# Encoder kernel, first layer: parts of w_in as one listed sequence, own buffers for early modulations, squares summed over pairs, splits one unit ahead

## The chip, the cores and the metric

One Trainium2 chip, one core of it, no communication. The metric is the time of one execution in device microseconds. The engines are TensorE (PE, matmuls; its weight loads are listed as PEld), VectorE (DVE), ScalarE (ACT), GpSimd (POOL) and SyncE (SP), whose queue issues all loads and stores.

## What is computed

Two layers of a bidirectional encoder for 256 tokens of width 2048, all in float32. Each layer modulates, mixes with two kinds of attention, gates, and runs a gated MLP with a short convolution. Cut to what matters:

```python
mod = silu(c) @ ada_w[l] + ada_b[l]                  # 2048 -> 6 x 2048: shift, scale, gate, twice
h = rmsnorm(x, norm_mix[l]) * (1.0 + sc_a) + sh_a
qa, ka, va, qb, kb, vb, ga, gb = split_cols(h @ w_in[l])      # 8704 columns
ya = window_attention(norm_rot(qa), norm_rot(ka), va, sink) @ w_proj_a[l]
yb = neighbourhood_attention(norm(qb), norm(kb), vb, bias) @ w_proj_b[l]
x = x + gt_a * ((sigmoid(ga) * ya + sigmoid(gb) * yb) @ w_out[l])
h = rmsnorm(x, norm_ffn[l]) * (1.0 + sc_m) + sh_m
g, v = split(depthwise_conv(h @ w_up[l]))
x = x + gt_m * ((silu(g) * v) @ w_down[l])
```

## The kernel before

**Weights.** All weights of a layer lie in one stream of 128 x 128 blocks in the order in which they are used (`block_stream`, line 74). Sixteen blocks are a unit, 1 MB. `unit` (L248) loads a unit (L253) into one of four `raw` tiles and splits each half of it into a high part (a cast to fp32r on ACT, L262) and a low part (a subtraction on DVE, L263); the two go into an `hl` tile, of which there are four, so two units. Every product is three matmuls: high x high, high x low, low x high. `Stream.next_block` (L292) asks for a unit when its first block is wanted.

**Two kinds of products.** `tokens` (L319) multiplies the 256 tokens with four neighbouring blocks of one row chunk: matmuls of 512 columns into two PSUM tiles, L329 to L331. `features` (L303) multiplies one block at a time, 256 columns, L271 to L273. The pool `mm` holds four PSUM tiles, the pool `ax` three more for everything else.

**Modulations.** `ada` (L184) makes one 128-wide piece of a modulation per step: a load of 1 MB (L193), which takes a `raw` tile too, and a fused multiply and sum on DVE (L194). There are 96 per layer; the first 32 are the shift and scale of the first h, in pairs by chunk of 128 channels. When both pieces of a chunk are there, `normed` (L415) makes that chunk of h: a product `ht` on DVE (L421), the high part on ACT (L424), the low part on DVE (L425). `plan` (L643) tells by a table of corners how many modulations are to be done when a unit of the stream ends.

**The first layer's start.** The sum of squares of x is made at L671 to L683: four squares on ACT, three adds and two halvings on DVE, two matmuls with a column of 1/D, an add of EPS on DVE. `roots` (L410) raises it to -0.5 on POOL, `spread` turns it into a row for all partitions by two transposes (L403) and a copy (L407): `rbs`, which `ht` needs.

**The first layer's w_in.** It has 13 column groups: nine of 512 columns for q, k and v (`QKV_GROUPS`) and 16 gate blocks of 128, run four rows of chunks at a time. The 16 chunks of the inner dimension are cut into four parts of 2, 4, 5 and 5 chunks (`K_PARTS_0`, L42); each part goes over all column groups before the next begins, so that work can start with two chunks of h. Between parts, sums wait in SBUF (`packs`, `ya`): the first part is copied there on ACT (L819, L855), later ones are added on DVE (L821, L850). A paced job, `ada_and_h` (L656), makes modulations and h chunks at 0.65 steps per unit, and what a part lacks when it begins is made at once (L806).

**Attention.** When a group of q and k is complete, `qk_rows` (L500) normalises it some ticks later; heads run as a paced job (`attention`, L782), whose steps are one per tick times a rate `ATT`. A head is scores (L584), softmax, four transposes (L610), a product with v (L618) and its split into `oA` or `oB`. `w_proj_a` (L862) starts after eight heads of A and reads all eight in each of its outputs.

The framework orders each engine's instructions by priority and by its own estimates; the rows in the section on the change are the outcome.

Of the kernel before, what the change touches and what calls it, by code (L numbers as in the profile page):

```python
# [32 lines left out]


# [84 lines left out]
def encoder(ctx: ExitStack, tc: tile.TileContext, a: dict, out: bass.AP):  # L119
# [25 lines left out]
    nc.vector.memset(mhalf[:], -0.5)  # L145
    def load(src, shape, name, p=const, **kw):
        t = p.tile(shape, F32, name=name, **kw)
        nc.sync.dma_start(t[:], src)
# [33 lines left out]
    mods, amods, nrms, done = {}, {}, {}, {0: 0, 1: 0}  # L182

    def ada(l):  # L184
# [6 lines left out]
        for n, i in enumerate(ADA_ORDER):  # L191
            raw = rawp.tile([P, D], F32, name=f"aw{l}_{n}", tag="raw")
            nc.sync.dma_start(raw[:], a["aw"][l, n])  # L193
            nc.vector.tensor_tensor_reduce(  # L194
                out=raw[:], in0=raw[:], in1=cact[:], scale=1.0, scalar=ab[:, i : i + 1],
# [52 lines left out]
    def unit(l, u):  # L248
# [4 lines left out]
        nc.sync.dma_start(raw[:], a["ws"][l, u])  # L253
# [828 lines left out]
```

## Time and profile before

| | us |
|---|---|
| median of 3 runs | 2689.32 (2689.2 to 2689.62) |
| the profiled execution | 2685.71 |
| its span, first to last instruction | 2683.2 |
| PE busy | 2647.0 |
| DVE busy | 2101.2 |
| ACT busy | 1393.7 |
| mean granted clock of TensorE | 0.997 |

The median is of unprofiled runs; all rows shown are of the profiled execution. A row of a timeline is: start, duration, engine, line, operation, output <- inputs, count, and in brackets the idle time of the engine just before and who ended it. A row of a group is: busy time, mean of one in ns, idle time before. Durations of neighbouring instructions of one engine overlap a little, and matmuls overlap by more than a third, so that the distance of starts, not the duration, is their rate. PE's busy share counts matmuls at reduced clock as busy; the granted clock stands beside it.

### The profile page before, as it was taken

To read this page: it belongs to the slowest core of one execution; us is meant where nothing else is said; L and a number is where in the kernel's file an instruction comes from. 1 tells how busy PE (TensorE), PEld (TensorE's weight loads), DVE (VectorE), ACT (ScalarE), POOL (GpSimd) and SP (SyncE) were. 2 spreads that over 40 slices of the span, in tenths; PEclk is the share of its full clock that TensorE was granted. 3 is DMA by queue.
4 is the path that set the end of the run, shared out by engine and by line. 5 is a ranking of instruction groups with operands and counts; after the bars stand their busy time and mean duration, and the time that the engine had idled before them with its cause. 6 is when DMAs were issued, how large, how long until landed. Compare 5 with 4: busy or idle time off the path is not lost.

```text
span 2683.2 us, 50732 instructions
## 1 busy us (share of the span) xinstructions
PE 2647.0 (99%) x21152; PEld 2559.6 (95%) x21152; DVE 2101.2 (78%) x2964; ACT 1393.7 (52%) x2266; POOL 36.3 (1%) x56
## 2 busy tenths in 40 slices
PE   7899999999999999999999999999999999999999
PEld 5689889999999999999998889999999999999999
DVE  6998988997988888788886666768878866655664
ACT  5344764455753555355554566544565445544553
POOL 0000100000000000000000000000000000000000
PEclk9999999999999999999999999999999999999999
DMA  8887768987688777887756656776747865555554
GB/s 320 333 341 290 269 234 326 357 322 250 233 286 336 291 269 281 325 303 269 294 213 256 242 219 228 245 260 245 291 173 282 300 252 191 196 195 190 193 199 142
DMA packets 104711, 700.40 MB, mean 261 GB/s; under 512 B 13473, under 2 KB 19873, under 8 KB 20513
## 3 DMA queue, kind: packets, MB, share of 16 engines
q1 hardware_dynamic: 104482, 697.18, 71.1%
q8 instruction: 165, 2.70, 0.4%
q14 instruction: 64, 0.52, 0.1%
HBM read 695.03 MB, written 2.10 MB: 260 GB/s over the span
## 4 chain that ended last, share of the span: by engine, by line
PE 92%; DVE 3%; DMA 2%; issue 1%; ACT 1%; POOL 0%; DVEq 0%; ACTq 0%
PE ps L271 25%; PE ps L273 25%; PE ps L272 25%; PE ps_t L330 5%; PE ps_t L331 5%; PE ps_t L329 5%; DMA aw<-in_aw 2%; DVE aw L194 1%; DVE hl L263 1%; PE sc L584 1%; PE po L618 1%; PE tp L610 1%; PE qtp L539 0%; PE cb L157 0%; ACT hl L262 0%
## 5 line engine op out<-in xcount | busy, mean ns | idle before, releaser
L263 DVE TENSOR_TENSOR hl<-w,hl 128x1024 fp32r<-128x1024 f32 x928 | 1127.7, 1222 | 315.4 <-ACT hl L262 314.2
L262 ACT CAST hl<-w 128x1024 fp32r<-128x1024 f32 x928 | 969.4, 1049 | 741.1 <-PE ps L273 446.8
L271 PE MATMUL ps<-h,hl 128*128 128x256 f32 x3328 | 924.5, 278 | 0.0
L273 PE MATMUL ps<-h,hl 128*128 128x256 f32 x3328 | 922.3, 277 | 0.0
L272 PE MATMUL ps<-h,hl 128*128 128x256 f32 x3328 | 921.6, 277 | 0.0
L271 PEld LDWEIGHTS ps<-h,hl 128*128 128x128 f32 x3328 | 626.0, 188 | 0.2
L272 PEld LDWEIGHTS ps<-h,hl 128*128 128x128 f32 x3328 | 625.2, 188 | 0.2
L273 PEld LDWEIGHTS ps<-h,hl 128*128 128x128 f32 x3328 | 625.1, 188 | 0.3 <-DVE hl L263 0.2
L194 DVE CUSTOM_DVE_ANT_0 aw<-aw,cact,ab 128x2048 f32<-128x2048 f32 x192 | 450.9, 2349 | 81.5 <-DMA aw<-in_aw 81.1
L329 PE MATMUL ps_t<-hl,h 128*128 128x512 f32 x576 | 227.7, 398 | 7.6 <-ACT hl L262 7.0
L330 PE MATMUL ps_t<-hl,h 128*128 128x512 f32 x576 | 227.0, 394 | 3.9 <-DVE hl L263 3.9
L331 PE MATMUL ps_t<-hl,h 128*128 128x512 f32 x576 | 226.2, 393 | 0.9 <-DVE h L425 0.9
L927 DVE SCALAR_TENSOR_TENSOR u<-ps,cw,u 128x255 f32<-128x255 f32 x304 | 146.4, 482 | 79.9 <-ACT u L925 75.4
L925 ACT ACTIVATE u<-ps,cw 128x256 f32<-128x256 f32 x152 | 85.6, 563 | 186.9 <-PE ps L273 186.9
L273 PE MATMUL ps<-merged,hl 128*128 128x256 f32 x512 | 141.7, 277 | 0.0
L272 PE MATMUL ps<-merged,hl 128*128 128x256 f32 x512 | 141.6, 277 | 0.0
L271 PE MATMUL ps<-merged,hl 128*128 128x256 f32 x512 | 141.6, 277 | 0.0
L273 PE MATMUL ps<-act_o,hl 128*128 128x256 f32 x512 | 141.5, 276 | 0.0
L272 PE MATMUL ps<-act_o,hl 128*128 128x256 f32 x512 | 141.5, 276 | 0.0
L271 PE MATMUL ps<-act_o,hl 128*128 128x256 f32 x512 | 141.2, 276 | 0.0
L329 PEld LDWEIGHTS ps_t<-hl,h 128*128 128x128 f32 x576 | 109.2, 190 | 31.0 <-ACT hl L262 7.6
L330 PEld LDWEIGHTS ps_t<-hl,h 128*128 128x128 f32 x576 | 109.1, 189 | 28.7 <-DVE hl L263 6.1
(213 smaller groups left out, 4579.6 us busy)
## 6 DMA issues: line engine op xcount, KB each, us to landing
w<-in_ws SPq DMA_DIRECT2D x464, 1024.0 KB, 4.9
aw<-in_aw SPq DMA_DIRECT2D x192, 1024.0 KB, 5.3
bias<-in_bias SPq DMA_DIRECT2D x64, 64.0 KB, 3.8
x<-in_xT SPq DMA_DIRECT2D x4, 512.0 KB, 5.2
out<-x SPq DMA_DIRECT2D x16, 128.0 KB, 2.2
cw<-in_cw SPq DMA_DIRECT2D x2, 176.0 KB, 3.2
maskA<-in_maskA SPq DMA_DIRECT2D x1, 256.0 KB, 5.7
ab<-in_ab SPq DMA_DIRECT2D x2, 48.0 KB, 5.4
```

What stands on the lines that cost most here:

```text
L194: nc.vector.tensor_tensor_reduce(out=raw[:], in0=raw[:], in1=cact[:], scale=1.0, scalar=ab[:, i : i + 1], op0=ALU.mult, op1=ALU.add, accum ...
L262: nc.scalar.copy(hl[:, 0], r)
L263: nc.vector.tensor_tensor(out=hl[:, 1], in0=r, in1=hl[:, 0].bitcast(F32), op=ALU.subtract)
L271: nc.tensor.matmul(out, hi, act[:, 0], start=first, stop=False)
L272: nc.tensor.matmul(ps[:, :S], hi, act[:, 1, :S], start=False, stop=False)
L273: nc.tensor.matmul(out, lo, act[:, 0], start=False, stop=last)
L329: nc.tensor.matmul(ps[:], xh, hi, start=kc == kcs[0], stop=False)
L330: nc.tensor.matmul(ps[:], xh, lo, start=False, stop=False)
L331: nc.tensor.matmul(ps[:], xl, hi, start=False, stop=kc == kcs[-1])
L584: nc.tensor.matmul(sc[:, t, :n], qT[:, t * P : (t + 1) * P], seen(t, kT), start=True, stop=True)
L925: nc.scalar.activation(out=u, in_=ps, func=AF.Identity, scale=w[:, 1:2], bias=w[:, 3:4])
L927: nc.vector.scalar_tensor_tensor(out=u[:, to], in0=ps[:, of], scalar=w[:, j : j + 1], in1=u[:, to], op0=ALU.mult, op1=ALU.add)
```

## The change

It concerns the first layer up to `w_proj_a`, and the pacing of modulations and heads.

1. The parts are gone. `ORDER` lists, for the first layer, turns of (column group, chunks to be reached); `turns` makes from it which chunks each turn adds. The gate blocks are four groups of four (groups 9 to 12). Groups reach different depths: the table begins with group 1 over chunks 0 and 1, group 0 over chunk 0, group 4 over 0 and 1, group 2 over 0 to 3; group 6 stops at chunk 1 until near the end. There are 33 turns of q, k and v in place of 36, and 12 turns of four gates in place of 16, so DVE has 48 adds of 512 columns in place of 54 and 32 of 256 in place of 48.
2. `need_h` makes each chunk of h with its two modulations when a turn asks for it, and `plan` makes chunks ahead; the paced job is gone. The corners of the plan now begin at unit 0.
3. The first three modulations of the first layer are loaded into space of `o` and `b1` (`own`), not into `raw` tiles. Unit 0 is issued after two modulations, in two loads of half a unit.
4. The squares of x: two on DVE, two on ACT; POOL adds the first two, DVE the last two; 16 matmuls of one column (8 for each half of the tokens) sum the rest in PSUM, and ACT adds EPS. A small power on POOL (`tried`) runs at the start. On ACT the four steps that make `cact` now stand ahead of the squares.
5. In the first layer up to unit 52 each unit's load and split are issued when the unit before begins (`SPLIT_AHEAD`).
6. The small tables (masks, gains, convolution weights) are loaded when the first group becomes complete, at unit 34, and no longer in the first unit.
7. `ATT` goes from 1.288 to 0.947 steps per tick, `ATT_B` from 0.21 to 0.296; heads of A may start when groups 0 to 2 are ready, heads of B when their own three are. Gates' sums of unfinished turns use `ax` PSUM tiles.

`SEEDED` is empty and `REDUCED` is 0, so the code that they guard is not built. `skip` is smaller by what `eps` and `tried` take, so addresses behind them stay. The instructions of the second layer's w_in and all later stages are the same, apart from where modulations fall among them.

```diff
-K_PARTS_0 = [2, 4, 5, 5]
+GATES = 4
+ORDER = [
+    [
+        (1, 2), (0, 1), (4, 2), (2, 4), (5, 3), (9, 3), (3, 2), (6, 2), (8, 3),
...
+    [(k, KC) for k in range(13)],
+]
-ADA_PLAN_0 = [(38, 32), (58, 48), (76, 66), (84, 70), (98, 80), (108, 80), (128, 88), (142, 99), (176, 113), (193, 126), (219, 136), (231, 143)]
+ADA_PLAN_0 = [(0, 3), (16, 18), (34, 32), (38, 32), (58, 48), (77, 67), (83, 70), (97, 80), (107, 80), (127, 86), (142, 99), (176, 111), (193, 126), (219, 139), (228, 142)]
-FIRST_RATE = 0.65
+OWN = 3
+SPLIT_AHEAD = 52
-ATT = [1.288, 0.4]
+ATT = [0.947, 0.4]
-ATT_B = [0.21, 0.21]
+ATT_B = [0.296, 0.21]
...
+    tried = const.tile([P, 1], F32, name="tried")
+    nc.gpsimd.tensor_tensor(out=tried[:], in0=mean[:], in1=mhalf[:, :1], op=ALU.pow)
...
-            raw = rawp.tile([P, D], F32, name=f"aw{l}_{n}", tag="raw")
+            raw = own.pop(0) if own else rawp.tile([P, D], F32, name=f"aw{l}_{n}", tag="raw")[:]
...
+        pieces = 1 if l or u else 2
...
-                if self.ahead:
-                    self.halves = self.ahead.popleft()
-                else:
-                    self.halves = unit(self.l, self.u)
+                if not self.ahead:
+                    self.prefetch(1)
+                self.halves = self.ahead.popleft()
                 self.u, self.at = self.u + 1, 0
+                if self.l == 0 and self.u < SPLIT_AHEAD:
+                    self.prefetch(1 - len(self.ahead))
...
+        if l == 0:
+            need_h(min(KC, (sum(done.values()) - 1) // 2))
...
+    def need_h(n):
+        while hs_done[0] < n:
+            need(0, 2 * hs_done[0] + 2)
+            next(hs_steps[0])
+            hs_done[0] += 1
...
+        if i < 8:
+            nc.vector.tensor_tensor(out=sq[:], in0=x[:, i : i + 4], in1=x[:, i : i + 4], op=ALU.mult)
+        else:
+            tc.keep_in_program_order(nc.scalar.activation(out=sq[:], in_=x[:, i : i + 4], func=AF.Square))
+        sqs.append(sq)
+    nc.gpsimd.tensor_tensor(out=sqs[0][:], in0=sqs[0][:], in1=sqs[1][:], op=ALU.add)
+    nc.vector.tensor_tensor(out=sqs[2][:], in0=sqs[2][:], in1=sqs[3][:], op=ALU.add)
...
-            todo = [(3, head_a, i) for i in range(HA)] + [(6 + 3 * (i // 4), head_b, i) for i in range(HB)]
+            todo = [({0, 1, 2}, head_a, i) for i in range(HA)]
+            todo += [({3, 4, 5} if i < 4 else {6, 7, 8}, head_b, i) for i in range(HB)]
...
+        for n, (k, kcs) in enumerate(turns(l)):
+            if l == 0:
+                need_h(kcs[-1] + 1)
+            if kcs[-1] == KC - 1 and not waits[0]:
+                gains, sink, cw, rots = small(l)
+                waits[0] = True
```

**How it moves instructions: three places.** First SP's queue at the start, before (`aw0_n` is the n-th modulation's weights, `w0_n` unit n of the first layer):

```order
L193 DMA aw0_0_145<-in_aw 128x2048
L193 DMA aw0_1_148<-in_aw 128x2048
L193 DMA aw0_2_170<-in_aw 128x2048
L193 DMA aw0_3_173<-in_aw 128x2048
L253 DMA w0_0_187<-in_ws 128x2048
L148 DMA maskA_207<-in_maskA 128x512
```

and now (`own_o` and `own_b1` are the modulations' own buffers):

```order
L230 DMA own_o_124<-in_aw 128x2048 x2
L293 DMA w0_0_169<-in_ws 128x1024 x2
L230 DMA own_b1_125<-in_aw 128x2048
L230 DMA aw0_3_202<-in_aw 128x2048
L293 DMA w0_1_212<-in_ws 128x2048
L293 DMA w0_2_252<-in_ws 128x2048
```

Unit 0 has moved ahead of the third and fourth modulation, units 1 and 2 follow at once, and the small tables are gone from here.

Second, DVE's list between the splits (`hl0_u_half`) of unit 6 and unit 7 before, with modulations 7 to 12 and three chunks of h:

```order
L263 TENSOR_TENSOR hl0_6_1_516<-w0_6_511,hl0_6_1_516 128x1024
L194 ISA aw0_7_550,mod0_139<-aw0_7_550,cact_94,ab0_140 128x2048
L194 ISA aw0_8_558,mod0_139<-aw0_8_558,cact_94,ab0_140 128x2048
L194 ISA aw0_9_561,mod0_139<-aw0_9_561,cact_94,ab0_140 128x2048
L194 ISA aw0_10_569,mod0_139<-aw0_10_569,cact_94,ab0_140 128x2048
L194 ISA aw0_11_572,mod0_139<-aw0_11_572,cact_94,ab0_140 128x2048
L194 ISA aw0_12_594,mod0_139<-aw0_12_594,cact_94,ab0_140 128x2048
L263 TENSOR_TENSOR hl0_7_0_599<-w0_7_597,hl0_7_0_599 128x1024
```

and now between the splits of units 2 and 3, and around that of unit 6 (small instructions left out):

```order
L303 TENSOR_TENSOR hl0_2_1_257<-w0_2_252,hl0_2_1_257 128x1024
L231 ISA aw0_4_268,mod0_158<-aw0_4_268,cact_98,ab0_159 128x2048
L231 ISA aw0_5_271,mod0_158<-aw0_5_271,cact_98,ab0_159 128x2048
L231 ISA aw0_6_279,mod0_158<-aw0_6_279,cact_98,ab0_159 128x2048
L231 ISA aw0_7_282,mod0_158<-aw0_7_282,cact_98,ab0_159 128x2048
L303 TENSOR_TENSOR hl0_3_0_312<-w0_3_310,hl0_3_0_312 128x1024
L303 TENSOR_TENSOR hl0_6_0_450<-w0_6_448,hl0_6_0_450 128x1024
L231 ISA aw0_8_470,mod0_158<-aw0_8_470,cact_98,ab0_159 128x2048
L303 TENSOR_TENSOR hl0_6_1_453<-w0_6_448,hl0_6_1_453 128x1024
L231 ISA aw0_9_473,mod0_158<-aw0_9_473,cact_98,ab0_159 128x2048
L303 TENSOR_TENSOR hl0_7_0_497<-w0_7_495,hl0_7_0_497 128x1024
```

The row of six modulations at unit 7 has become a row of four ahead of unit 3, and from there on one or two stand between splits.

Third, PE's list in `w_proj_a` (`ps0_u_..` is an output whose last block lies in unit u, `oA0_6` and `oA0_7` heads 6 and 7, `tp` a head's transposes, `sc` its scores, `po` its product with v). Before:

```order
L610 MATMUL tp_3080<-ident_85,p_3052 128x128
L618 MATMUL po_3183<-pT_3085,vh_2946 128x256 x6
L271 MATMUL ps0_52_16_0_3353<-oA0_6_2968,hl0_52_0_3356 128x256
L271 MATMUL ps0_53_8_0_3387<-oA0_6_2968,hl0_52_1_3359 128x256
L271 MATMUL ps0_53_16_0_3460<-oA0_6_2968,hl0_53_0_3463 128x256
L271 MATMUL ps0_54_8_0_3494<-oA0_6_2968,hl0_53_1_3466 128x256
L610 MATMUL tp_3192<-ident_85,p_3089 128x128
L618 MATMUL po_3305<-pT_3197,vh_2946 128x256 x6
L271 MATMUL ps0_52_16_0_3353<-oA0_7_3070,hl0_52_0_3356 128x256
```

and now:

```order
L311 MATMUL ps0_52_16_0_3326<-oA0_6_2963,hl0_52_0_3329 128x256
L311 MATMUL ps0_53_8_0_3360<-oA0_0_2362,hl0_52_1_3332 128x256
L311 MATMUL ps0_53_8_0_3360<-oA0_6_2963,hl0_52_1_3332 128x256
L662 MATMUL tp_3247<-ident_85,p_3158 128x128
L670 MATMUL po_3283<-pT_3252,vh_2941 128x256 x5
L311 MATMUL ps0_54_8_0_3423<-oA0_0_2362,hl0_53_1_3395 128x256
L311 MATMUL ps0_52_16_0_3326<-oA0_7_3074,hl0_52_0_3329 128x256
```

Before, four outputs were open, all of them short of head 6, when the transposes and the product of head 6 stood in the list, and then again for head 7. Now head 6's product stands ahead of the first output's last blocks, and three outputs are open when head 7 comes.

More of the change, by code (lines that the diff above doesn't have):

```diff
@@ L182, in encoder @@
     mods, amods, nrms, done = {}, {}, {}, {0: 0, 1: 0}
+    own = []
+    for tag, n in (("o", 16), ("b1", 12)):
+        t = place(tag, n, F32, f"own_{tag}").rearrange("p n s -> p (n s)")
+        own += [t[:, i : i + D] for i in range(0, n * S - D + 1, D)]
+    own = own[:OWN]
     def ada(l):
@@ L654, in need @@
             next(adas)
-    def ada_and_h(steps):
-        for kc in range(KC):
-            while done[0] < 2 * kc + 1:
-                next(adas)
-                yield
-            next(adas)
-            next(steps)
-            yield
-    for _ in range(FIRST):
-        next(adas)
-    for i in range(0, KC, 4):
-        nc.sync.dma_start(x[:, i : i + 4], a["xT"][:, i : i + 4])
-    mean_sq = sm.tile([P, 2], F32, name="ms_in", tag="nsa")
-    acc = place("y0", 4, F32, "sq_in")
-    for i in range(0, KC, 4):
-        sq = acc if i == 0 else place(f"y{1 + i // 4 % 2}", 4, F32, f"sq_in{i}")
-        nc.scalar.activation(out=sq[:], in_=x[:, i : i + 4], func=AF.Square)
-        if i:
-            nc.vector.tensor_tensor(out=acc[:], in0=acc[:], in1=sq[:], op=ALU.add)
@@ new lines, in encoder @@
+    nc.gpsimd.tensor_tensor(out=sqs[0][:], in0=sqs[0][:], in1=sqs[1][:], op=ALU.add)
+    nc.vector.tensor_tensor(out=sqs[2][:], in0=sqs[2][:], in1=sqs[3][:], op=ALU.add)
+    pss = [ax.tile([P, 2], F32, name="ss_in", tag="ss", bufs=1), ax.tile([P, 512], F32, name="ss_in1", tag="ax")]
+    for sq in sqs[::2]:
+        for t in range(2):
+            for i in range(4):
+                nc.tensor.matmul(
+                    pss[t][:, :1], sq[:, i, t * P : (t + 1) * P], mean[:],
+                    start=sq is sqs[0] and i == 0, stop=sq is sqs[2] and i == 3,
+                )
@@ L681, in encoder @@
     for t in range(2):
-        nc.tensor.matmul(ps[:, t : t + 1], acc[:, 0, t * P : (t + 1) * P], mean[:], start=True, stop=True)
-    nc.vector.tensor_scalar(out=mean_sq[:], in0=ps[:], scalar1=EPS, scalar2=None, op0=ALU.add)
+        nc.scalar.activation(out=mean_sq[:, t : t + 1], in_=pss[t][:, :1], func=AF.Identity, bias=eps[:])
     tables = []
@@ L746, in va @@
             return vas[g]
-        ready, heads = [0], [0]
+        ready, heads = set(), [0]
         oA, oB = [], []
@@ new lines, in gate, with gate_a @@
+        def gate(n, mo, kcs):
+            first, last = kcs[0] == 0, kcs[-1] == KC - 1
+            apart = l == 0 and not waits[0]
+            seeded = apart and n in SEEDED and not first
+            if not apart:
+                clean[0] = False
+            def gate_a(ps):
+                src = ps
+                if not first and not seeded:
+                    nc.vector.tensor_tensor(out=ya[:, mo], in0=ps, in1=ya[:, mo], op=ALU.add)
+                    src = ya[:, mo]
+                if last:
+                    half_tanh(ya[:, mo], src)
+                elif first or seeded:
+                    nc.scalar.copy(ya[:, mo], ps)
+            st.features([hs[k] for k in kcs], [gate_a], apart=apart, seed=ya[:, mo] if seeded else None)
```

172 lines of the change are left out of this document (97 added, 75 removed), and 4 rows, old and new, of the table ORDER.

## The prediction

> **What bounds the kernel now.** I read the page's first lines, then a table of windows with one row for each stage, then the waits, and for the two stages that lose time the timeline. The page gives the span:
>
> ```profile
> span 2683.2 us, 50732 instructions
> PE 2647.0 (99%) x21152; PEld 2559.6 (95%) x21152; DVE 2101.2 (78%) x2964; ACT 1393.7 (52%) x2266; POOL 36.3 (1%) x56
> aw<-in_aw SPq DMA_DIRECT2D x192, 1024.0 KB, 5.3
> ```
>
> The windows by stage (stretch in us, its length, busy time of each engine with instructions, granted clock, DMA share, GB/s) say where the 36 us are that PE is not busy:
>
> ```profile
> 0.00:26.00 26.00, 11.52 (x26) 6.21 (x26) 13.83 (x19) 10.32 (x13) 3.57 (x7) 1.00 0.93 353
> 26.00:67.00 41.00, 39.12 (x207) 32.99 (x206) 31.49 (x42) 28.15 (x49) 0.00 (x0) 0.96 0.80 298
> 67.00:82.00 15.00, 5.35 (x17) 3.00 (x17) 14.89 (x20) 3.78 (x6) 0.00 (x0) 0.75 0.98 374
> 82.00:276.00 194.00, 193.11 (x1053) 168.18 (x1052) 183.46 (x242) 86.81 (x139) 7.06 (x4) 0.99 0.84 316
> 276.00:349.00 73.00, 72.41 (x479) 64.94 (x478) 71.41 (x139) 56.75 (x150) 7.98 (x4) 1.00 0.70 259
> 349.00:418.00 69.00, 64.39 (x507) 61.22 (x506) 58.57 (x123) 40.19 (x93) 2.08 (x14) 0.98 0.69 250
> 418.00:2683.00 2265.00, 2261.15 (x18876) 2223.07 (x18875) 1727.60 (x2384) 1167.70 (x1821) 15.59 (x28) 1.00 0.70 254
> ```
>
> After 418 us PE idles under 4 us in 2265, and the change leaves the order there nearly alone; the gain or loss is made before. PE idles at the start (no product of w_in before 26), in 67 to 82 (5.35 busy of 15, clock 0.75, while DVE is full with 14.89), and in 349 to 418 (4.6 idle). DVE is nearly full from 67 to 349. The rate of PE, from neighbouring starts, first at full clock and then after the long stop:
>
> ```profile
> 37.24 0.39 PE L329 MATMUL ps_t<-hl,h 128*128 128x512 f32 x1
> 37.47 0.39 PE L330 MATMUL ps_t<-hl,h 128*128 128x512 f32 x1
> ...
> 66.94 0.39 PE L329 MATMUL ps_t<-hl,h 128*128 128x512 f32 x1
> ...
> 69.42 0.39 PE L330 MATMUL ps_t<-hl,h 128*128 128x512 f32 x1
> 69.65 0.39 PE L329 MATMUL ps_t<-hl,h 128*128 128x512 f32 x1
> ...
> 71.21 0.73 PE L331 MATMUL ps_t<-hl,h 128*128 128x512 f32 x2 [0.93 <-DVE h L425]
> 78.93 1.22 PE L329 MATMUL ps_t<-hl,h 128*128 128x512 f32 x2 [6.99 <-ACT hl L262]
> 81.26 0.80 PE L330 MATMUL ps_t<-hl,h 128*128 128x512 f32 x1 [1.11 <-DVE hl L263]
> ...
> 82.71 0.63 PE L331 MATMUL ps_t<-hl,h 128*128 128x512 f32 x1
> 83.14 0.63 PE L329 MATMUL ps_t<-hl,h 128*128 128x512 f32 x1
> ```
>
> A matmul starts every 0.23 us, and every 0.43 after the stop. A unit of 16 blocks has 24 of them: 5.5 us (48 of half the length for gates: the same). The row at 66.94 is the first of the second part, 6.5 units in. From there 17 matmuls (3.9 us) take 15 us, and the next 8 run at half rate: 11.1 + 1.6 = **12.7 us lost**. The cause is the five modulations in a row on DVE.
>
> **The change part by part.** Rows for the prices (line, operation, count, then busy us, mean ns), the last two of POOL and ACT:
>
> ```profile
> L263 DVE TENSOR_TENSOR hl<-w,hl 128x1024 fp32r<-128x1024 f32 x118 | 142.3, 1220 | 14.3 <-ACT hl L262 14.2
> L194 DVE CUSTOM_DVE_ANT_0 aw<-aw,cact,ab 128x2048 f32<-128x2048 f32 x49 | 115.0, 2346 | 0.1
> L821 DVE TENSOR_TENSOR packB<-ps_t,packB 128x512 f32<-128x512 f32 x36 | 23.7, 686 | 1.4 <-PE ps_t L331 1.4
> L850 DVE TENSOR_TENSOR ya<-ps,ya 128x256 f32<-128x256 f32 x48 | 19.7, 419 | 1.5 <-PE ps L273 1.4
> L425 DVE SCALAR_TENSOR_TENSOR h<-ht,mod,h 128x256 fp32r<-128x256 f32 x16 | 7.7, 482 | 0.7 <-ACT h L424 0.7
> masks.py:199 POOL TENSOR_SCALAR_AFFINE_SELECT ident<-ident 128x128 f32<-128x128 f32 x1 | 0.3, 292 | 0.1
> L412 POOL TENSOR_TENSOR nrs<-nss,mhalf 128x2 f32<-128x2 f32 x3 | 2.1, 696 | 1144.1 <-DVE nss L475 1144.1
> L599 ACT ACTIVATE es<-nm,sink 128x2 f32<-128x2 f32 x8 | 2.3, 285 | 0.0
> ```
>
> In a row of DVE work each next one starts about 0.08 before the last ends, so I count 1.14, 2.27, 0.61, 0.34 and 0.40. And the start, from the timelines of ACT, DVE, PE and POOL:
>
> ```profile
> 10.70 1.99 ACT L675 ACTIVATE sq_in<-x 128x1024 f32<-128x1024 f32 x2
> 17.73 1.01 PE L682 MATMUL ss_in<-mean,sq_in 128*128 128x1 f32 x4 [7.56 <-DVE sq_in L679]
> 20.06 2.35 DVE L194 CUSTOM_DVE_ANT_0 aw<-aw,cact,ab 128x2048 f32<-128x2048 f32 x1
> 20.10 2.87 POOL L412 TENSOR_TENSOR nrs<-ms_in,mhalf 128x2 f32<-128x2 f32 x1 [18.80 <-DVE ms_in L683]
> 23.03 0.69 PE L403 MATMUL rb<-ident,nrs 128*128 128x128 f32 x2 [4.29 <-POOL nrs L412]
> 23.75 0.37 ACT L407 COPY rbs<-rb 128x256 f32<-128x256 f32 x1 [11.06 <-PE rb L403]
> 29.09 0.50 PE L330 MATMUL ps_t<-hl,h 128*128 128x512 f32 x1 [1.88 <-DVE hl L263]
> ```
>
> *First squares.* The last square on ACT still ends at 12.7, since the four cact steps before it depend on PE. Then: one add on DVE (1.2, to 13.9); eight matmuls in place of two, of which the trace has 4 passes in 1.01 us, so 16 passes 4.0 (to 17.9; the other eight run earlier); `ms_in` on ACT 0.3; the power 0.7; `rb` 0.7; the copy 0.4; six hand-offs of 0.1. That is 20.6, against 24.1 now: 3.5 earlier. Gone are two reductions by halves and the wait of `ms_in` behind a modulation on DVE. Bounds: 16 passes that overlap as far as the 128-wide row at 23.03 can't show, 1.0 to 4.0; I keep 4.0. The power took 2.87 here and 0.70 in its three later uses; I take 0.70, and 2.87 is the other end (start 2.2 later).
>
> The 2.87 can be a first use, which `tried` would absorb, or a wait: the row of DVE's modulation at 20.06 ends at 22.41, 0.56 before the power. [...] The later 0.70s fit either reading.
>
> *The add of the first two squares on POOL* (1024 columns) has no row in the trace. The AFFINE_SELECT row, 0.29 for 128, scaled by 8 gives 2.3; the same add on DVE 1.2 is the lower bound, two inputs at twice the select 4.7 the upper. It starts at about 7.6, after DVE's second square; its cover is ACT's squares and DVE's add until 13.9, less the 4.0 of its own matmuls. Up to 2.3 costs nothing; 4.7 costs 2.4. [...]
>
> *Own buffers and order of loads.* Weights of unit 0 are issued behind two modulations and not four, in two halves, and need no slot: at the first window's 353 GB/s the 4.5 MB up to its first half take 13 us, so it is there long before 20. So the cast of its first half (1.0) follows `rbs` at once: 21.6; subtraction 22.8; PE flows from there, against 29.1: 6.3 earlier, into the same cold clock.
>
> *What is late next* is h of chunks 1, 2 and 3. DVE now does hl0_0_1 (to 24.4), then six modulations (13.6), four splits of units 1 and 2 (4.6), three times amod, ht and h's low half (2.8), and two waits for ACT's half of h (1.0): 46.4. Splits of unit 3 follow, so **unit 3 starts at about 47.7**. PE has 72 matmuls until then, 16.6 us and 3.2 for the cold clock, in 25 us: it waits some 5 us, in three pieces (before h1 about 1, h2 2, h3 2). So unit 6.5 is reached at 47.7 + 3.5 x 5.5 = 67, exactly as now: the earlier start is spent on four modulations more. But these are then done, and the stop at 67 is not there.
>
> *Units 6.5 to 36.* Pairs of modulations still stand ahead of the splits of units 8 and 10 and around 13 to 15. Going down DVE's list in this way, h4 comes at 65 (needed at 65), h5 at 75 (needed at 74), h6 at 88.5 (needed at 87), h7 and h8 at 113 and 116 (needed at 115 and 116). I allow 2.5 us of waits: 12.7 - 2.5 = a lead of **10 us**. From unit 10 DVE has slack: ahead of the split of unit 21 stand 44 splits, 21 modulations, 14 + 13 adds and 10 h, 125 us, and with the waits so far it gets there at 144, PE at 149. Upper bound 12, lower 4 (waits of 8). Splits one unit ahead cost nothing while two units of hl exist: a cast waits for PE to leave the unit before, and evacuations behind it on ACT wait as long, which four PSUM tiles cover. Adds: 54 to 48 and 48 to 32, 6 x 0.61 + 16 x 0.34 = 9 us of DVE, with no wait of PE behind them except in the tail. The small tables' loads stand on SP ahead of the second weights now:
>
> ```profile
> 17.74 0.43 SPq L148 DMA_DIRECT2D maskA<-in_maskA  x1
> ...
> 20.92 0.38 SPq L253 DMA_DIRECT2D w<-in_ws  x1
> ```
>
> They hold SP 3.2 us; moved to unit 34 they hold the weights of unit 35 as long, whose split is due a unit ahead (5.5 us of PE), and DVE for 1 us: nothing.
>
> *The tail, 349 to 418.* The rows of the stop:
>
> ```profile
> 362.00:368.00 6.00, 4.69 (x31) 3.88 (x32) 3.27 (x14) 2.98 (x10) 0.30 (x2) 1.00 0.50 175
> 368.00:374.00 6.00, 3.77 (x19) 3.12 (x19) 3.94 (x8) 4.03 (x14) 0.00 (x0) 0.80 0.64 206
> 374.00:380.00 6.00, 5.15 (x35) 4.55 (x34) 4.70 (x14) 5.66 (x12) 0.30 (x2) 0.92 0.18 59
> ```
>
> Idle 4.4 and slow clock 1.7: 6.1. Here all four PSUM tiles of w_proj_a stand in PE's queue before heads 6 and 7 are done. In the new order the same heads stand about one unit earlier. DVE idles here too, so room exists; I take **5 us**, bounds 0 (DVE, 71.41 of 73 before it, holds the heads back as much) and 10.
>
> Sum: 10 + 5 = 15. The profiled execution took 2685.7 (2683.2 and 2.5 around it), 3.6 under the median of 2689.3; I take the difference off the median: **2674**.
>
> **The rivals.** *DVE sets the tail.* Between the splits of units 44 and 52 it has 59 us of work by the new order, 56 by the old; then 44 against 51. If it is the bound, the tail gives 0 to -2 at best and the front's lead loses 2: -8, 2681. For: 71.41 of 73. Against: its idle 6 us in 362 to 380.
>
> *The clock falls in the waits for h1 to h3.* Each fall costs 16 x 0.2 = 3.2 us, as after 78.93. With two falls and later h the front gives 2, the tail 5: 2682. Against: the short waits at 69 to 71 left the spacing at 0.23 (69.42, 69.65).
>
> *Slower: modulations that land late.* They and the weights share four slots and one queue, now with pairs ahead of splits; each us by which one lands after its place on DVE holds all splits behind it, with one unit in hand. Fourteen stand before unit 16: break-even with the 15 is 1.1 us each; at 1.5 it is +6, 2695. For: landing takes 5.3 in the median, twice a reduction. Against: idle before modulations is 0.1 in the row of 49.
>
> *It does nothing.* The lead is lost in waits for h and DVE keeps the tail: 2688. *More:* no waits after unit 3 and a closed tail: 12.7 + 10 = 23, 2666.
>
> **How the numbers follow.** Forecast (-10 to -20) 0.55; DVE's tail 0.22; clock 0.08; late landings 0.06; nothing 0.05; more 0.04. A measurement of this kernel can tell about 0.2%, 5.4 us. Faster by more: 0.55 + 0.04 and most of the tail and clock cases, 0.23 of 0.30: 0.82. Same: 0.12. Slower: 0.06. The range from 2664 (the gains' upper bounds and start 2 us better) to 2686 (both at their lower bounds) leaves out the slower case and most of "nothing".
>
> **What would show it.** Right: first flow at 22 to 24, unit 3 near 48, no wait of PE over 3 us in 60 to 90 and clock 1.00 there, first product with oA near 339, last near 402. Wrong: `rbs` after 22.5 (squares or POOL), unit 10 after 95 (h chain), waits for aw before DVE's modulations (late landings), or the tail still 69 us from first to last product with oA.

## The result and the profile after

The changed kernel takes 2670.78 us in the median of four runs (2669.16 to 2673.14), the kernel before 2689.47 on the same chip (2689.2 to 2691.25): 18.7 us less, a ratio of 0.993 with a 95% interval of 0.9913 to 0.9947. On a second chip the two kernels ran again: 2670.95 and 2686.83, a ratio of 0.9936 (0.992 to 0.9953). The forecast was 2674, its range 2664 to 2686. The profiled execution after took 2671.87, span 2669.9; against the one before, the span is 13.3 us shorter.

The page's first line after, then the same windows by stage as before (stretch in us, its length, busy time of PE, PEld, DVE, ACT and POOL with instructions, granted clock, DMA share, GB/s):

```profile
span 2669.9 us, 50770 instructions
```

```profile
0.00:26.00 26.00, 21.29 (x68) 15.35 (x69) 14.26 (x20) 9.84 (x15) 4.50 (x9) 1.00 0.92 364
26.00:67.00 41.00, 34.71 (x151) 27.56 (x151) 33.77 (x37) 22.89 (x35) 0.00 (x0) 0.92 0.80 305
67.00:82.00 15.00, 13.60 (x93) 12.43 (x92) 13.48 (x18) 8.72 (x15) 0.00 (x0) 1.00 0.98 357
82.00:276.00 194.00, 193.10 (x1017) 165.64 (x1016) 183.08 (x247) 94.53 (x181) 11.71 (x6) 1.00 0.85 319
276.00:349.00 73.00, 72.78 (x549) 68.32 (x548) 71.58 (x144) 54.66 (x134) 2.77 (x3) 1.00 0.76 277
349.00:418.00 69.00, 68.39 (x580) 67.53 (x579) 58.17 (x109) 38.62 (x79) 2.09 (x14) 1.00 0.77 289
418.00:2669.00 2251.00, 2246.95 (x18733) 2208.59 (x18732) 1718.51 (x2372) 1159.93 (x1808) 15.35 (x26) 1.00 0.69 254
```

Three rows differ from those before. The stretch 67 to 82 is nearly full (13.60 of 15 at clock 1.00, was 5.35 at 0.75): the stop is gone. The stretch 26 to 67 has become worse (34.71 at 0.92, was 39.12 at 0.96). In 349 to 418 PE is busy for 68.39 in place of 64.39. From 276 to 349 it was full and is full, yet with 549 matmuls in place of 479: 54 of the 70 more belong to the weight stream, which here has more matmuls of 256 columns and fewer of 512, and 16 to the heads; more on this below.

Windows at fixed times compare different work. So I also lined up the two traces by work: each 512-wide matmul of the weight stream counts as 1/24 of a unit, each 256-wide one as 1/48, and the start times of the first matmul at the same count are subtracted. This gives a *lead* over the kernel before, in us, at each unit. All leads in the text come from this; the first row of the table below is the time at which the kernel before gets there.

```
unit             0.5    3   6.5     8    36    48    54    60    75   median less before's
before at       32.6 47.1  66.9  88.1 243.8 316.1 376.0 417.6 505.5
after            7.1 -2.5  -2.5   8.5   8.7   2.6  15.7  16.8  14.7   -18.7
after_again      7.0 -1.7  -2.3   8.7   8.9   2.9  15.6  16.7  14.7   -15.9
no_ahead         7.5 -5.7  -5.3   7.3   5.2  -2.0  10.7  10.7  10.5   -10.6
old_squares      3.4 -3.4  -3.0   8.0   8.2   2.1  15.2  16.3  14.3   -14.6
no_own           7.6 -1.1  -0.7  10.3  10.5   4.4  17.7  18.8  16.7   -14.7
no_tried         7.4 -2.5  -2.2   8.8   9.0   2.9  16.1  17.2  15.1   (one run)
old_parts        3.2  3.6   3.8  10.3   8.4   8.5   6.2   6.7   6.5    -5.4
no_plan          6.8 -1.8  -2.4   8.6  -0.3  -6.5   6.1   7.3   5.2    -9.6
old_pace         7.5 -1.4  -1.0  10.0  10.3   4.4  14.8   9.2  12.4   -13.9
before_pace     -0.4  0.1   0.1  -0.8  -0.8  -1.2   2.9   3.9   2.8    -2.7
parts_early      3.3  3.7   3.9  10.8   8.6   2.0  15.2  15.2  10.1   -10.4
still_earlier    7.5 -1.2  -0.8  10.2  10.4   0.4  14.1  17.5  14.6   -15.4
light_tail       6.8 -2.8  -2.8   8.2   8.4   2.3  13.5  12.8  -3.6    +5.6
```

The names are those of the experiments below. Two rows say how finely this can be read: up to unit 36 still_earlier is the same program as after, and its lead there is 10.4 against 8.7. The clock makes this difference. PE's waits from 21 to 70 us are nearly the same (6.6 and 6.3 us), but the granted clock was at half for 3.4 us once in still_earlier (from 42.29) and twice in after (from 30.00 and from 47.07), and 3.4 us at half the rate cost 1.7. In the same way after_again and light_tail, with two such stretches, have 8.9 and 8.4, and old_pace, with one, has 10.3. So single executions differ by up to 2 us, and smaller differences in this table say nothing unless the clock is taken into account. The lead at unit 75 agrees with the difference of the medians within 4.4 us in every row; in light_tail the loss goes on past it.

The row "after" is the story: 7 us ahead half a unit in, 2.5 behind at unit 3, 8.5 ahead when the stop is passed, the same at unit 36 (8.7), 2.6 at unit 48, 15.7 at unit 54, 14.7 at unit 75 and after. The front brings 8.7 us and the tail 6.0.

**The start after**, from the timelines of POOL, DVE, ACT and PE (start, duration, then what):

```profile
8.09 2.34 POOL L728 TENSOR_TENSOR sq_in<-sq_in,sq_in 128x1024 f32<-128x1024 f32 x1 [6.25 <-DVE sq_in L724]
17.84 0.93 POOL L459 TENSOR_TENSOR nrs<-ms_in,mhalf 128x2 f32<-128x2 f32 x1 [7.42 <-ACT ms_in L739]
...
12.43 1.23 DVE L729 TENSOR_TENSOR sq_in<-sq_in,sq_in 128x1024 f32<-128x1024 f32 x1 [4.42 <-ACT sq_in L726]
15.85 2.35 DVE L231 CUSTOM_DVE_ANT_0 own_o<-own_o,cact,ab 128x2048 f32<-128x2048 f32 x1
...
19.55 0.37 ACT L454 COPY rbs<-rb 128x256 f32<-128x256 f32 x1 [1.78 <-PE rb L450]
...
21.72 0.77 PE L376 MATMUL ps_t<-hl,h 128*128 128x512 f32 x1
```

`rbs` is ready at 19.92, and the first product of w_in starts at 21.72. Then PE's waits for the second, third and fourth chunk of h, and its clock behind them; again PE's timeline:

```profile
29.50 0.50 PE L376 MATMUL ps_t<-hl,h 128*128 128x512 f32 x1 [2.36 <-ACT h L471]
...
31.05 0.63 PE L377 MATMUL ps_t<-hl,h 128*128 128x512 f32 x1
31.47 0.63 PE L378 MATMUL ps_t<-hl,h 128*128 128x512 f32 x1
...
41.30 0.49 PE L376 MATMUL ps_t<-hl,h 128*128 128x512 f32 x1 [1.58 <-ACT h L471]
41.64 0.39 PE L377 MATMUL ps_t<-hl,h 128*128 128x512 f32 x1
41.87 0.40 PE L376 MATMUL ps_t<-hl,h 128*128 128x512 f32 x1
...
46.96 0.72 PE L376 MATMUL ps_t<-hl,h 128*128 128x512 f32 x1 [2.33 <-ACT h L471]
...
78.11 0.38 PE L311 MATMUL ps<-h,hl 128*128 128x256 f32 x1 [1.41 <-ACT hl L302]
```

The three waits in brackets are 2.36, 1.58 and 2.33. Behind the two long ones matmuls start 0.43 apart (31.05, 31.47, and again from 47.48 on), behind the short one 0.23 (41.64, 41.87). At 78.11 stands the one wait that is left where the stop of 7 us was.

**The tail after.** The windows of the first to the last product with `oA`, and of two stretches that lay in the stop before:

```profile
362.00:368.00 6.00, 5.89 (x49) 5.72 (x50) 5.91 (x14) 4.08 (x9) 0.30 (x2) 1.00 0.53 194
368.00:374.00 6.00, 6.00 (x54) 6.00 (x54) 6.00 (x8) 3.44 (x9) 0.00 (x0) 1.00 0.80 270
344.40:398.90 54.50, 53.89 (x454) 52.94 (x453) 48.77 (x97) 31.35 (x68) 1.60 (x11) 1.00 0.75 275
```

The products with `oA` run from 344.5 to 399.1, 54.6 us in place of 68, and PE is full in them.

### The profile page after: what moved, and what is told of

It is laid out like the page before. It is cut to its first block, busy times and chain, and to the rows that moved or that the text cites. A ratio compares the mean times of both kernels' runs of the same rounds, so it can differ in the third digit from the quotient of the medians.

```text
span 2669.9 us, 50770 instructions
## 1 busy us (share of the span) xinstructions
PE 2650.8 (99%) x21180; PEld 2565.4 (96%) x21180; DVE 2092.8 (78%) x2940; ACT 1389.2 (52%) x2265; POOL 36.4 (1%) x58
## 4 chain that ended last, share of the span: by engine, by line
PE 95%; DVE 3%; DMA 1%; ACT 1%; issue 1%; POOL 0%; SPq 0%; DVEq 0%
PE ps L311 26%; PE ps L313 26%; PE ps L312 26%; PE ps_t L377 4%; PE ps_t L378 4%; PE ps_t L376 4%; DVE aw L231 1%; PE sc L636 1%; PE po L670 1%; DVE hl L303 1%; DMA aw<-in_aw 1%; PE tp L662 1%; PE qtp L591 0%; ACT hl L302 0%; PE ss_in L734 0%
## 5 line engine op out<-in xcount | busy, mean ns | idle before, releaser
L231 DVE CUSTOM_DVE_ANT_0 aw<-aw,cact,ab 128x2048 f32<-128x2048 f32 x189 | 443.8, 2349 | 58.6 <-DMA aw<-in_aw 57.9
## 6 DMA issues: line engine op xcount, KB each, us to landing
w<-in_ws SPq DMA_DIRECT2D x2, 512.0 KB, 10.5
```

The costliest lines, as they stand in the source:

```text
L231: nc.vector.tensor_tensor_reduce(out=raw, in0=raw, in1=cact[:], scale=1.0, scalar=ab[:, i : i + 1], op0=ALU.mult, op1=ALU.add, accum_out=m ...
```

## Experiments

Theory at the outset: the front's lead comes from modulations that are no longer made in rows, and the tail's from heads that come a unit earlier. Rivals were that the earlier start (squares, own buffers) carries the front, that the heads' pace alone carries the tail, and that DVE bounds the tail. The kernel before ran beside every group of runs: medians 2685.67 (old_pace, old_parts, no_ahead, before_pace), 2686.83 (after_again, no_own, old_squares, light_tail), 2687.7 (parts_early, no_tried) and 2686.55 (no_plan, still_earlier).

### The changed kernel again

> The changed kernel once more, as the measure for the runs beside it on the same chip. 12 to 19 us under the kernel before; nothing is told apart by it alone.

No edit. Measured 2670.95 (2667.84 to 2674.7), ratio 0.9936 (0.992 to 0.9953). The gain holds on a second chip.

### The front: the start

No buffers of their own for the first three modulations:

```diff
-OWN = 3
+OWN = 0
```

> The changed kernel with the first three modulations in raw tiles (OWN 0). The loads of the fourth modulation and of units 1 and 2 then wait for tiles; by the rows of the changed kernel they still land ahead of their place on DVE, so within 1.5 us of the changed kernel. If own buffers are what brings h1 early: the wait of PE before h1 grows from 2.5 to over 5 us and the time by 3.

Measured 2672.09 (2668.51 to 2673.37), ratio 0.9942 (0.9927 to 0.9957); its lead at unit 36 is 10.5, not less than the change's. The own buffers bring nothing that shows.

The squares as they were (four on ACT, adds and halvings on DVE, two matmuls, EPS on DVE):

```diff
-    sqs = []
+    acc = place("y0", 4, F32, "sq_in")
...
+        nc.scalar.activation(out=sq[:], in_=x[:, i : i + 4], func=AF.Square)
+        if i:
+            nc.vector.tensor_tensor(out=acc[:], in0=acc[:], in1=sq[:], op=ALU.add)
+    for n in (2, 1):
+        nc.vector.tensor_tensor(out=acc[:, :n], in0=acc[:, :n], in1=acc[:, n : 2 * n], op=ALU.add)
```

> The changed kernel with the old sum of squares (four squares on ACT, adds and halvings on DVE, two matmuls). If the start sets all of the chain of h up to chunk 3, as in my prediction: rbs 3 to 4 us later, unit 3 later by as much, and the time 3 to 4 us longer. If the later rbs is covered, because modulations that are there run on DVE in the meantime: under 1.5 us.

Measured 2672.26 (2670.93 to 2677.39), ratio 0.9949 (0.9934 to 0.9963); after_again on the same chip is 1.3 us faster, and the two ranges overlap. The first `ht`, which needs `rbs`, starts at 23.14 in place of 19.95, and the lead at unit 0.5 is 3.7 smaller; at unit 3 it is 0.9 smaller, at unit 36 0.5. PE's timeline shows one reason:

```profile
31.57 0.50 PE L376 MATMUL ps_t<-hl,h 128*128 128x512 f32 x1 [0.71 <-ACT h L471]
43.37 0.49 PE L376 MATMUL ps_t<-hl,h 128*128 128x512 f32 x1 [2.61 <-ACT h L471]
```

With a later start the wait for the second chunk of h is 0.71 in place of 2.36: part of an earlier start is only waited away. But not all of it. DVE's `ht` of the second chunk, in the changed kernel and here:

```profile
28.43 0.48 DVE L468 SCALAR_TENSOR_TENSOR ht<-x,amod,rbs 128x256 f32<-128x256 f32 x1
...
30.48 0.49 DVE L468 SCALAR_TENSOR_TENSOR ht<-x,amod,rbs 128x256 f32<-128x256 f32 x1
```

It comes 2.05 later here, and those of the third and fourth chunk 2.06 and 2.07 later. So of the 3.19 us of the start 2.1 stay in the chain of h; the other 1.1 are one split of unit 0, which DVE makes here while it waits for `rbs`. That the lead is only 0.5 smaller at unit 36 is the clock: it was at half for 3.4 us once here before unit 8 and twice in the changed kernel's trace. Against still_earlier, the same program as the change with one such stretch, the lead at unit 36 is 2.2 smaller. So the new squares bring about 2 us at an equal clock, and a difference of the medians of 1.3 that is not clear of the noise.

The small power at the start replaced by a memset:

```diff
-    nc.gpsimd.tensor_tensor(out=tried[:], in0=mean[:], in1=mhalf[:, :1], op=ALU.pow)
+    nc.gpsimd.memset(tried[:], 0.0)
```

> The changed kernel without the early power on POOL (a fill in its place). If the 2.87 us of the first power before were a first use: the power that gives rbs takes 2.5 to 3 us in place of 0.93, and rbs comes 2 us later. If they were a wait for DVE's modulation: it stays at 0.6 to 1.0 and ends 0.56 after the modulation beside it.

One run, 2669.64. The timelines of POOL and DVE:

```profile
17.60 1.10 POOL L459 TENSOR_TENSOR nrs<-ms_in,mhalf 128x2 f32<-128x2 f32 x1 [7.68 <-ACT ms_in L739]
...
15.79 2.35 DVE L231 CUSTOM_DVE_ANT_0 own_o<-own_o,cact,ab 128x2048 f32<-128x2048 f32 x1
```

Without a power ahead of it, `nrs` takes 1.10, not 2.87, and it ends at 18.70, 0.56 after DVE's modulation (18.14). With `tried` it takes 0.93 and ends 0.57 after the modulation. So the first-use reading falls: the 2.87 of before, which ends 0.56 after the modulation beside it too, fits the wait.

### The front: splits ahead, list and plan

Splits not ahead of their unit:

```diff
-SPLIT_AHEAD = 52
+SPLIT_AHEAD = 0
```

> The changed kernel without splits one unit ahead (SPLIT_AHEAD 0). By my prediction they cost and bring nothing while two units of hl exist: within 2 us of 2671. If they are what keeps PE fed while modulations stand on DVE: waits of PE for hl of some 0.5 us in many of the units 8 to 20, and 2677 to 2681.

Measured 2675.07 (2673.77 to 2677.04), ratio 0.9956 (0.9939 to 0.9972). The time lies between the two readings of the expectation. The lead at unit 3 is 3.2 smaller than after's, at unit 36 3.5, at unit 75 4.2. PE's timeline has a wait that the changed kernel has not, for a cast of weights (second row):

```profile
38.59 0.59 PE L376 MATMUL ps_t<-hl,h 128*128 128x512 f32 x1 [2.78 <-ACT h L471]
45.17 1.22 PE L376 MATMUL ps_t<-hl,h 128*128 128x512 f32 x2 [3.24 <-ACT hl L302]
```

Here the split of a unit is asked for only when its first block is wanted, and PE stands at the unit's edge until it is made. Splits ahead are worth some 3.5 us up to unit 36.

The old four parts written as a list, all else as in the change:

```diff
-    [
-        (1, 2), (0, 1), (4, 2), (2, 4), (5, 3), (9, 3), (3, 2), (6, 2), (8, 3),
...
-    ],
+    [(k, n) for n in (2, 6, 11, 16) for k in range(13)],
```

> The changed kernel whose list of turns is the four old parts (all 13 groups over chunks 0 and 1, then over 2 to 5, 6 to 10, 11 to 15); modulations by the new plan, splits ahead, new squares and pace stay. If the smooth plan of modulations does it: some 9 of the 12 modulations that the second part wants are done when it begins, three are made at once, and PE stops 5 to 7 us there; time 2675 to 2678. If the list itself does it: a stop of 12 us as before and 2681 to 2684. If neither list nor plan matters: no stop over 3 us and 2669 to 2673.

Measured 2680.32 (2678.61 to 2683.7), ratio 0.9976 (0.9965 to 0.9987). The lead at unit 36 is 8.4, as with the new list: **the front's gain does not need the list**. In place of early waits this kernel has 4.2 us of waits at 68 to 75, where the second part begins, and half the clock from 72 to 79. The tail's gain is gone: 8.4 at unit 36, 6.5 at unit 75; so the time lies between what the two theories gave. The window of the stop in w_proj_a:

```profile
352.00:374.00 22.00, 17.14 (x90) 14.39 (x89) 15.31 (x40) 12.78 (x32) 0.89 (x6) 0.77 0.53 187
```

PE idles for nearly 5 us and the clock is 0.77; DVE idles too (15.31 of 22).

The new list without the first corners of the plan, so that a chunk of h is made only when a turn asks for it:

```diff
-ADA_PLAN_0 = [(0, 3), (16, 18), (34, 32), (38, 32), (58, 48), ...
+ADA_PLAN_0 = [(38, 32), (58, 48), ...
```

> This is the changed kernel without the three first corners of the plan, so that a chunk of h and its two modulations are made only when a turn of the list asks for it. Theory P (the plan that makes chunks ahead brings the front's lead): modulations come in rows of two to six ahead of the turns, PE stops 2 to 5 us at several of them, the worst where the list steps by three chunks (group 7 over chunks 12 to 14, near unit 30); the lead over the kernel before at unit 36, 8.5 us, falls to 0 to 4, and the median is 4 to 8 us above the changed kernel's. Rival L (the list itself spreads the modulations, since it steps by one or two chunks nearly everywhere): the lead at unit 36 stays at 7 or more and the median within 2 us of the changed kernel's.

Measured 2677.0 (2676.25 to 2684.28), ratio 0.9967 (0.9954 to 0.9979). Neither theory has it whole. Up to unit 28 the lead is as good as with the plan (7.0 against 7.5): the list, which steps by one or two chunks, spreads the modulations by itself. It steps by three chunks once, and there 7.3 us are lost (lead 7.0 at unit 28, -0.3 at unit 36): 4.1 of waits, and 3.2 by half the clock behind them (218.40 to 225.22, PE busy for 6.42 of it). The traced execution (2684.28) is the slowest of the six; by the medians the plan's corners are worth some 6 us (9.6 under the kernel before, against after_again's 15.9 on another chip). PE's and DVE's timelines at the place:

```profile
213.64 0.73 PE L378 MATMUL ps_t<-hl,h 128*128 128x512 f32 x2 [0.93 <-DVE h L472]
216.92 0.50 PE L376 MATMUL ps_t<-hl,h 128*128 128x512 f32 x1 [2.54 <-ACT h L471]
...
208.17 2.34 DVE L231 CUSTOM_DVE_ANT_0 aw<-aw,cact,ab 128x2048 f32<-128x2048 f32 x1
210.84 2.34 DVE L231 CUSTOM_DVE_ANT_0 aw<-aw,cact,ab 128x2048 f32<-128x2048 f32 x1
213.57 2.34 DVE L231 CUSTOM_DVE_ANT_0 aw<-aw,cact,ab 128x2048 f32<-128x2048 f32 x1
216.24 2.34 DVE L231 CUSTOM_DVE_ANT_0 aw<-aw,cact,ab 128x2048 f32<-128x2048 f32 x1
```

This is the old stop at 67 in small: modulations in a row on DVE, and PE behind them. So the front needs small steps, from the list or from the plan, and the plan covers the places where the list steps far.

### The tail: pace, heads, modulations

The old pace of the heads in the changed kernel:

```diff
-ATT = [0.947, 0.4]
+ATT = [1.288, 0.4]
...
-ATT_B = [0.296, 0.21]
+ATT_B = [0.21, 0.21]
```

> The changed kernel with the old pace of heads (ATT 1.288, ATT_B 0.21). If the pace of the heads is what closed the stop in w_proj_a: the stretch from the first to the last product with oA goes from 55 us back to 64 to 68, and the time to 2679 to 2683. If the tail gained because DVE has less work and arrives earlier: the stretch stays under 58 and the time within 3 us of 2671.

Measured 2671.79 (2671.24 to 2674.03), ratio 0.9942 (0.9928 to 0.9957). The two signs of the expectation part: the stretch of the products with `oA` is 64.8 us, as the first theory had it, and the time is that of the second. The stretch's window:

```profile
341.50:406.30 64.80, 62.81 (x499) 60.36 (x498) 56.19 (x125) 38.66 (x88) 2.38 (x16) 0.97 0.65 228
```

PE idles for 2.0 us in it, against 4.6 in the kernel before (349.3 to 417.5), and the clock is at half once for 3.4 us. The rest of the 10 us by which it is longer than the change's stretch is work: 499 matmuls in place of 456. So the stop stays closed but for some 3 us (14.8 at unit 54). The pace moves work of the heads of B between units 54 and 66 (9.2 at unit 60 against 16.8), and by unit 75 little of that is left (12.4 against 14.7).

The new pace in the kernel before, whose tables of pace are the only edit:

```diff
-ATT = [1.288, 0.4]
+ATT = [0.947, 0.4]
...
-ATT_B = [0.21, 0.21]
+ATT_B = [0.296, 0.21]
```

> The kernel before with nothing but the new pace of heads (ATT 0.947, ATT_B 0.296). If the pace closes the stop in w_proj_a by itself: from first to last product with oA 58 to 62 us in place of 68, and a time of 2680 to 2684. If the stop closed through the new order of groups: no change, 2687 to 2691.

Measured 2682.99 (2680.34 to 2685.77), ratio 0.9987 (0.9977 to 0.9996). Both signs of the first theory came: the time lies in its range, and the stretch of the products with `oA` is 60.1 us.

```profile
351.80:411.90 60.10, 58.08 (x474) 55.88 (x472) 53.62 (x113) 35.11 (x80) 1.79 (x12) 1.00 0.75 278
```

PE idles for 2.0 us in it in place of 4.6. The lead is 3.9 at unit 60, 2.8 at unit 75 and 1.3 at unit 100. So the pace alone closes part of the stop and is worth 2.7 us by the medians (1.1 to 6.2 by the interval), against some 6 for the tail of the change; in the changed kernel, where the heads come earlier anyway, the old pace costs nothing that is clear of the noise.

The old parts with each group's normalising put off by two ticks in place of three, which brings the heads one unit forward:

```diff
-    [
...
+    [(k, n) for n in (2, 6, 11, 16) for k in range(13)],
...
-PUT_OFF = 3
+PUT_OFF = 2
```

> The run with the old four parts in the list, and one edit more: the norms of q and k one tick earlier (PUT_OFF 2), so that the heads stand one unit earlier on PE, about where the new list has them. If the stop in w_proj_a closes because heads 6 and 7 come a unit earlier: unit 54 starts 6 us or more earlier than in that run, and the time falls from 6 us under the kernel before to 10 to 13. If the list closes it by spreading the work of DVE: unit 54 moves less than 2 us.

Measured 2677.33 (2673.87 to 2680.86), ratio 0.9966 (0.9951 to 0.998). The product with v of the last head but one, which stood at unit 53.5 with the old parts, stands at unit 52.0, and the lead at unit 54 is 15.2 in place of 6.2. **The stop closes because the heads come a unit earlier**, whatever the list. In the list it comes from groups 0, 1 and 2, which are complete at unit 38.0 in place of 39.5 (the 14 units of 56 chunk steps that follow them in the table, against the 12.5 of the last old part). But here the lead falls again from 15.2 at unit 60 to 7.8 at unit 66, and 10.1 is left at unit 75; why more is given back than in the changed kernel stays open.

The same edit on the changed kernel:

```diff
-PUT_OFF = 3
+PUT_OFF = 2
```

> This is the changed kernel with the normalising of a group of q and k put off by two ticks in place of three, so that the heads of A start one unit earlier again. Theory M (PE is full in units 42 to 48, the heads' matmuls that come into it take its time one for one, and the gain is only the stop in w_proj_a, which is closed already): the lead at unit 48 falls from 2.6 us by 2 to 4, the lead at unit 54 stays at 16, within 1.5, and the median within 2 us of the changed kernel's. Rival S (slack of the heads is still what w_proj_a waits for): the lead at unit 54 rises by 2 us or more and the median falls by as much.

Measured 2671.14 (2669.22 to 2675.5), ratio 0.9945 (0.993 to 0.996). The lead at unit 48 falls from 2.6 to 0.4, at unit 54 it is 14.1 against 15.7, at unit 75 14.6 against 14.7: the same kernel time. Once the stop is closed, earlier heads are only work moved.

What is moved shows in PE's groups for units 44 to 48; of the stream's lines one of three is shown, of the heads' the product with v. The kernel before, 290.2 to 316.1:

```profile
L329 PE MATMUL ps_t<-hl,h 128*128 128x512 f32 x24 | 9.6, 402 | 0.0
L271 PE MATMUL ps<-h,hl 128*128 128x256 f32 x17 | 4.7, 277 | 0.0
L618 PE MATMUL po<-pT,vh 128*128 128x256 f32 x6 | 1.1, 300 | 0.0
```

The changed kernel, the same units, 282.6 to 313.5:

```profile
L311 PE MATMUL ps<-h,hl 128*128 128x256 f32 x49 | 13.9, 285 | 0.0
L376 PE MATMUL ps_t<-hl,h 128*128 128x512 f32 x8 | 3.3, 415 | 0.0
L670 PE MATMUL po<-pT,vh 128*128 128x256 f32 x18 | 2.6, 281 | 0.0
```

The stream's four units take the same PE time in both (4 x 5.5 = 22). Of 25.9 us that leaves 3.9 for 28 rows of heads (149 rows in all less the stream's 121), of 30.9 it leaves 8.9 for 60 (229 less 169). PE is full in both; so the 5 us that units 44 to 48 "lose" are the heads' matmuls that no longer stand in the stop.

Modulations put off past the stretch of the heads:

```diff
-ADA_PLAN_0 = [(0, 3), (16, 18), (34, 32), (38, 32), (58, 48), (77, 67), ...
+ADA_PLAN_0 = [(0, 3), (16, 18), (34, 32), (38, 32), (52, 36), (60, 46), (77, 67), ...
```

> The changed kernel with fewer modulations on DVE in units 38 to 52 (36 done at unit 52 in place of 43, 46 at unit 60, the rest by unit 77 as now). If DVE sets the units 42 to 52, where the lead over the kernel before fell from 8.5 to 3 us: the lead at unit 50 is 6 us or more and the time 3 to 5 us under the changed kernel. If the heads' own chain sets it: no change there, and what is put off costs up to 3 us later.

Measured 2692.4 (2689.03 to 2693.8), ratio 1.0021 (1.0012 to 1.003): slower than the kernel before. The leads up to unit 48 are those of the changed kernel (2.3), so DVE's modulations do not set the pace of the heads. The cost behind was far above what either theory expected: from 12.8 at unit 60 to -7.4 at unit 100. The windows of 425 to 470 and of 470 to 520, and the largest of PE's waits from 320 to 540 (us in total, times, longest):

```profile
425.00:470.00 45.00, 39.28 (x327) 37.59 (x325) 36.34 (x44) 18.78 (x30) 0.00 (x0) 1.00 0.93 353
470.00:520.00 50.00, 47.31 (x382) 46.85 (x382) 41.55 (x43) 16.88 (x24) 0.00 (x0) 0.93 0.94 366
```

```profile
PE ps L311 <- ACT hl L302: 6.5, 4, 1.9
```

PE waits for casts while DMA is busy for 0.93 of the time. By the new corners each unit from 52 on asks for 1 MB of weights and 1.25 MB of modulations, 2.36 million bytes; at 353 to 366 GB/s that takes 6.4 to 6.7 us, more than PE's 5.5. That the rate of loads is the bound is worked out from these rows, not shown by a run of its own, and it is not the only reading. The changed kernel, which asks for 1 MB and 1 MB, has 387 GB/s at a DMA share of 0.99 in its own window 425 to 470, more than here. The rival is that both kinds of loads share four `raw` tiles, so that a load goes out only when DVE has freed one; no run tells the two apart. Some 3.5 us of the loss are the clock (0.93 of the 50 us).

## Why the prediction was right, and where it was not

- **The start.** `rbs` was forecast at 20.6 and came at 19.92; POOL's add was put at 2.3 and took 2.34, under the cover named. DVE's own add of 1024 columns took 1.23, so POOL's took 1.90 times as long. The power was taken at 0.70; it took 0.93, and ended 0.57 after the modulation of DVE beside it (18.20). The first product came at 21.72, forecast 22.8. The 3.2 us put down for a cold clock behind it are a term that no run shows; in its place three starts lay 0.57, 0.48 and 0.42 apart, then 0.24, which is 0.8.
- **The start is spent on more modulations.** Right in the main: the change is 7.1 us ahead at half a unit and 2.5 behind at unit 3. What the new squares give to it is small: without them the chain of h is 2.1 later, of 3.2 at its first `ht`. The own buffers bring nothing that shows.
- **h1 to h3.** Waits of about 1, 2 and 2 us, in sum 5, were forecast; the three brackets are 2.36, 1.58 and 2.33, in sum 6.3. Unit 3 began at 49.6, forecast 47.7, and unit 6.5 at 69.4, forecast 67. Part of this is the rival with the clock, which I gave 0.08 and 3.2 us a fall: the clock fell twice. Each fall lasted 3.4 us, so it cost 1.7, about half of my price. That price, 16 starts "as after 78.93", misread the rows: behind 78.93 they show 8 at the slow rate, which the prediction itself counts as 1.6 us. So the start came 2.4 cheaper than priced, and the two falls cost 3.4 that the sum did not have: two errors that partly cancel.
- **The stop at 67 to 82 gone, 2.5 us of waits after it.** Right: the one wait between 60 and 90 is the 1.41 at 78.11, and the clock is 1.00. The front's lead was forecast at 10 (bounds 4 to 12) and is 8.7: unit 6.5 is 2.5 us late, and the waits behind it are 1.1 shorter than the 2.5 allowed.
- **Splits ahead "cost nothing".** The step was mis-sized: they were given no gain either, and are worth 3.5 us of the 8.7. The count down DVE's list held their gain without naming it, since it used the order as it stood.
- **The tail.** The mechanism was right (heads a unit earlier, the stop closes, DVE has room) and its price too, 5 forecast and 6.0 measured. Its times were not: the first product with `oA` came at 344.5 and not 339, the last at 399.1 and not 402. The step that failed is that units 36 to 52 would keep the front's lead; the heads' matmuls moved into them and took 5 us there, and the stop gave back more than the 5 allowed (15.7 - 6.6 = 9.1 between units 53 and 54; the lead at unit 53 was 6.6).
- **DVE sets the tail** (0.22): it does not. From 344.4 to 398.9 PE is busy 53.89 of 54.5 and DVE 48.77, and light_tail left units 42 to 48 as they were.
- **Late landings, nothing**: DVE's waits for loads of modulations sum to 0.7 us up to 420, by its groups.
- **The sum.** 15 forecast, 14.7 measured at unit 75. That it is so close is partly luck: the front came 1.3 short and the tail 1.0 over, and the clock alone moves the front by 1.7 from one execution to the next. The difference of the medians is 18.7 on one chip and 15.9 on another; the profiled execution before was 3.6 below its median and the one after 1.1 above, and leads move by 2 to 4 us late in the program (after: 15.7 at unit 350, 13.3 at unit 400), where only the places of modulations differ. That part has no cause that a run here shows. The fewer adds on DVE and the later load of the small tables, which the prediction put at nothing, had no run of their own.

## What to carry to other kernels

When several things are made ahead of the engine that must not wait, look at the engine that makes them: here five modulations of 2.35 us in a row on DVE stopped PE (5.35 us busy of the 15 from 67 to 82), and the same work in steps of one or two, with the next weights' split ahead of it, did not (13.60 of 15). An earlier start is worth what it moves of the chain behind it, here 2.1 us of 3.2; the rest is waited away. Closing the stop moved its work to where PE was already full (5 us into units 44 to 48), so measure at a point behind both places; and before work is put off, count the bytes per unit that it then needs.
